# A decoder layer on one core: at two norm boundaries, 512 columns of x come at once and the rest in stages

## The chip, the cores and the metric

The kernel runs on one core of a Trainium2 chip. The time is that of one execution on the device, in microseconds (us), as the median of three runs. A profile is taken of one further execution.

## The reference

One layer of a decoder is computed for a batch of 1, 256 tokens, a width of 2048 and an FFN width of 5632, all in float32. Shortened to what matters:

```
h = rms_norm(x, ln_mix_pre)
proj = h @ w_in
o = heads(proj)
x = x + rms_norm(o @ w_out, ln_mix_post)
h = rms_norm(x, ln_ffn_pre)
g, u = split(h @ w_gate_up)
f = (silu(g) * u) @ w_down
x = x + rms_norm(f, ln_ffn_post)
gate = sigmoid(rms_norm(x, ln_pli) @ w_pli_gate)
x = x + gate * (p @ w_pli_proj)
```

Twice a norm over all 2048 columns lies between two matrix products: after w_out (the norm is added to x, and x is what w_gate_up multiplies) and after w_down (x is what w_pli_gate multiplies). These are called the FFN boundary and the gate boundary below. The scale of the norm ahead of a product is one number per token, so the kernel applies it to the product's result and multiplies only the gain into x.

## The kernel before

The 256 tokens are two tiles of 128 (t = 0 and 1). A product's accumulator is one PSUM bank of 128 tokens by 512 columns; there are eight banks. Every float32 operand is split into a high and a low part (`split`, L108: ScalarE casts the high part, VectorE subtracts it from the raw value), and a product of two is three matmuls: high by high, high by low, low by high. So one block of 128 rows of a weight costs three matmuls of 512 columns for each t.

Weights come from HBM on SyncE's queue into `wraw`, are split into `whi` and `wlo`, and each of these three has three buffers of 128x4x512. `gemm` (L178) with `Chunk` (L133) runs a product of 512 columns: chunks of four row blocks, with t = 0 and 1 taking turns every two row blocks; `front` chunks at the start and `tail` chunks at the end are run for t = 0 first and then for t = 1, so that t = 0 starts early or ends early.

The order on each engine is set by the Tile framework's scheduler: by default it follows the program's order; what is written under `tc.high_priority` is put ahead by the given number of places (200 for weight loads and their splits, 1000 for chains that end a product). The engines then run their lists in order and wait for each other through semaphores.

At a boundary `post_norm` (L243) runs for each t, from the last evacuation of the product (`evac_out`, L566, and `evac_down`, L810). VectorE multiplies the last 512 columns by the gain (L571 or L822), sums the squares (L246), GpSimd takes the power -1/2 (`rsqrt`, L216, tile `rs`), and then, for each of four groups of 512 columns: VectorE adds the normed product to x (L250), TensorE transposes the group in four matmuls against an identity (`split_T`, L235, into banks 4 and 5), VectorE multiplies by the next gain (L240), and ScalarE and VectorE split the result into `hT_hi` and `hT_lo` (L109 and L110). Each of these is 128x512. `hT` is what the next product multiplies; row blocks 0 to 3 of the weight need group 0, 4 to 7 group 1, and so on.

To give TensorE something to do meanwhile, half of p @ w_pli_proj is run at each boundary (`embed`, L590, two `gemm`s of two row blocks each: 24 matmuls, of `pT`). Its results are kept in memory (`pp_d`) until the end, and so is x (`x_d`, L605).

After the FFN boundary `unit_first` (L729) computes the first 512 of 5632 gate and up columns. Its weights come as `Pair` objects (L642): two row blocks of the gate columns and two of the up columns in one `whi`/`wlo` buffer. The first two pairs are run for t = 0 and then t = 1, the other six with both t. `differences` (L608) makes operands that only the later units use; its pieces are queued with `later` and released by `tick`. Ten more units (L755), and in three parts the products with w_down, follow. After the gate boundary come four `gemm`s of 512 columns with w_pli_gate, of 16 row blocks each, the first with one chunk of `front`, and `evac_gate` (L848), which ends in the output's stores.

Of the kernel before, what the change touches and what calls it, by code (L numbers as in the profile page):

```python
# [10 lines left out]
F32 = mybir.dt.float32  # L11
BF16 = mybir.dt.bfloat16
F32R = mybir.dt.float32r
# [4 lines left out]
T = 2  # L18
# [18 lines left out]
def kernel(  # L37
# [205 lines left out]
    def post_norm(hT, x_sb, t, ssy, gain):  # L243
# [4 lines left out]
        for c in range(4):  # L248
# [3 lines left out]
            split_T(hT, x_sb, t, c, gain)  # L252

# [4 lines left out]
    with tc.tile_pool(name="mixed", bufs=1) as mixed:  # L258
# [307 lines left out]
        def evac_out(n, last):  # L566
            def evac(t, pm):
# [21 lines left out]

    def embed(n, ring, out):  # L590

        gemm((pT_hi, pT_lo), w_pli_proj, 0, 2, n * NB, out, ring=ring)

    def embed_out(n):
        def evac(t, pm):
            pp = temp()
            nc.scalar.copy(pp, pm)
            nc.gpsimd.dma_start(out=pp_d[:, (2 * t + n) * NB:(2 * t + n + 1) * NB], in_=pp)
        return evac
# [42 lines left out]
    class Pair:  # L642


        def __init__(self, j, i, seven):
            self.i, self.seven = i, seven
            with tc.high_priority(offset=WEIGHT_AHEAD):
                raw, hi, lo = w_tiles()
                rows = slice(i * 2 * P, (i + 1) * 2 * P)
                for n0, sl in ((DFF + j * NB, slice(0, 4, 3)), (j * NB, slice(1, 3))):  # L650
                    nc.sync.dma_start(
                        out=raw[:, sl], in_=w_gate_up[rows, n0:n0 + NB].rearrange("(c q) n -> q c n", q=P))
# [41 lines left out]
        def first(self, m):  # L694

            t, n = {2: (0, 0), 3: (0, 1), 4: (1, 0), 5: (1, 1)}[m]
            return [([x[:, 2 * self.i + c, t, :] for x in hT], [x[:, k, :] for x in self.w])
                    for c, k in enumerate(((1, 2), (0, 3))[n])]
# [4 lines left out]
    def accumulate(m, terms, first, last):  # L703
        for x, (a, w) in enumerate(terms):
            for y, (u, v) in enumerate(((0, 0), (0, 1), (1, 0))):
                nc.tensor.matmul(  # L706
                    bank[M[m]], lhsT=a[u], rhs=w[v], start=first and x == 0 and y == 0,
                    stop=last and x == len(terms) - 1 and y == 2)

    def hidden(fT, k, t, f):  # L710
# [18 lines left out]
    def unit_first(j, fT, k):  # L729

        n = len(PAIRS)
        pairs = [Pair(j, i, False) for i in range(2)]
        for ms in ((2, 3), (4, 5)):
            for i in range(2):
                for m in ms:
# [189 lines left out]
```

## Time and profile before

| what | value |
|---|---|
| median of 3 runs | 1270.91 us (1270.76 to 1270.93) |
| the profiled execution's own time | 1270.12 us |
| its span, first to last instruction | 1268.4 us |
| TensorE (PE) busy | 1246.9 us, 98% |
| VectorE (DVE) busy | 828.6 us, 65% |
| ScalarE (ACT) busy | 613.7 us, 48% |
| GpSimd (POOL) busy | 28.3 us, 2% |
| DMA | 245.08 MB, 193 GB/s over the span |

The profiled execution's time is the span and 1.7 us around it. The times of the rows are us from the span's start. PE's busy share is high because matmuls overlap: a matmul's row lasts longer than the distance to the next one's start, so a stretch is best read by the starts of its matmuls. A row's "idle before" names the instruction that ended the wait.

### The profile page before, as it was taken

What the parts mean: (1) busy time and instruction counts of PE and PEld (TensorE: products, weight loads), DVE (VectorE), ACT (ScalarE), POOL (GpSimd) and SP (SyncE); (2) the same over time, 40 slices, a digit from 0 to 9 for tenths busy, and PEclk for the clock granted to TensorE, in tenths of its full rate; (3) what the DMA queues carried; (4) which work ended last, traced back from release to release, by engine and by line L of the source; (5) the groups of instructions that cost most, each with busy time, mean ns of one, the idle gap of its engine ahead of it and who ended that gap; (6) DMA issues with size and microseconds to landing.
All of it is one profiled execution on the core that took longest, in us unless ns stands there. A gap on an engine that the chain in (4) does not pass through costs nothing.

```text
span 1268.4 us, 14080 instructions
## 1 busy us (share of the span) xinstructions
PE 1246.9 (98%) x5554; PEld 1003.9 (79%) x5554; DVE 828.6 (65%) x812; ACT 613.7 (48%) x683; POOL 28.3 (2%) x53
## 2 busy tenths in 40 slices
PE   9999999999999899999999999999999999997998
PEld 6887888888887688888888888888888888886886
DVE  6574665555545957987535798886457988657543
ACT  6654554445443745555433555553334555446332
POOL 0001000000100100000000000000000000001000
PEclk9999999999999899999999999999999999998999
DMA  9754745454754655556555555556555555843661
GB/s 341 265 165 163 239 151 167 165 166 166 246 190 161 238 194 170 185 189 220 199 186 178 189 186 189 201 176 222 197 174 185 188 188 185 314 163 133 235 210 53
DMA packets 121810, 245.08 MB, mean 193 GB/s; under 512 B 6112, under 2 KB 6416, under 8 KB 120848
## 3 DMA queue, kind: packets, MB, share of 16 engines
q1 hardware_dynamic: 119536, 233.07, 54.4%
q0 software_dynamic: 1952, 11.02, 2.3%
q8 instruction: 43, 0.70, 0.2%
q14 instruction: 23, 0.19, 0.0%
q10 hardware_dynamic: 256, 0.10, 0.0%
HBM read 238.91 MB, written 6.83 MB: 194 GB/s over the span
## 4 chain that ended last, share of the span: by engine, by line
PE 93%; DVE 3%; ACT 2%; issue 1%; DMA 1%; POOL 0%; ACTq 0%; DVEq 0%; POOLq 0%
PE bank L159 52%; PE bank L706 37%; ACT whi L109 1%; DVE wlo L110 1%; PE bank L715 1%; PE bank L367 1%; DMA wraw<-in_w_in_dram 1%; PE bank L337 1%; DVE x_sb L250 0%; DVE hT_lo L110 0%; ACT hT_hi L109 0%; DMA gT<-in_gains_dram 0%; PE bank L380 0%; PE bank L379 0%; PE bank L378 0%
## 5 line engine op out<-in xcount | busy, mean ns | idle before, releaser
L110 DVE TENSOR_TENSOR wlo<-wraw,whi 128x2048 fp32r<-128x2048 f32 (+2 forms) x237 | 475.1, 2014 | 322.0 <-ACT whi L109 321.7
L109 ACT CAST whi<-wraw 128x2048 fp32r<-128x2048 f32 (+2 forms) x237 | 398.5, 1688 | 435.3 <-PE bank L159 250.6
L159 PE MATMUL bank<-whi,hT_hi 128*128 128x512 f32 x512 | 207.9, 407 | 1.1 <-ACT whi L109 1.1
L159 PE MATMUL bank<-wlo,hT_hi 128*128 128x512 f32 x512 | 203.5, 397 | 1.6 <-DVE wlo L110 1.5
L159 PE MATMUL bank<-whi,hT_lo 128*128 128x512 f32 x512 | 203.3, 397 | 0.0
L706 PE MATMUL bank<-wlo,hT_hi 128*128 128x512 f32 x454 | 180.8, 398 | 4.1 <-DVE wlo L110 4.1
L706 PE MATMUL bank<-whi,hT_lo 128*128 128x512 f32 x454 | 180.0, 397 | 0.0
L706 PE MATMUL bank<-whi,hT_hi 128*128 128x512 f32 x454 | 179.1, 399 | 0.3 <-ACT hT_hi L109 0.3
L159 PE MATMUL bank<-whi,fT_hi 128*128 128x512 f32 x352 | 139.8, 397 | 0.0
L159 PE MATMUL bank<-wlo,fT_hi 128*128 128x512 f32 x352 | 139.2, 395 | 0.0
L159 PE MATMUL bank<-whi,fT_lo 128*128 128x512 f32 x352 | 139.2, 395 | 0.0
L159 PEld LDWEIGHTS bank<-whi,hT_lo 128*128 128x128 f32 x512 | 96.8, 189 | 23.5 <-DVE hT_lo L284 0.2
L159 PEld LDWEIGHTS bank<-wlo,hT_hi 128*128 128x128 f32 x512 | 96.9, 189 | 22.8 <-DVE wlo L110 2.9
L159 PEld LDWEIGHTS bank<-whi,hT_hi 128*128 128x128 f32 x512 | 96.8, 189 | 22.7 <-ACT whi L109 1.6
L706 PEld LDWEIGHTS bank<-wlo,hT_hi 128*128 128x128 f32 x454 | 85.7, 189 | 26.1 <-DVE wlo L110 6.5
L706 PEld LDWEIGHTS bank<-whi,hT_lo 128*128 128x128 f32 x454 | 85.7, 189 | 20.3
L706 PEld LDWEIGHTS bank<-whi,hT_hi 128*128 128x128 f32 x454 | 85.5, 189 | 20.4 <-ACT hT_hi L109 0.5
L666 DVE TENSOR_TENSOR wlo<-wsum,whi 128x2048 fp32r<-128x2048 f32 x30 | 68.7, 2290 | 24.8 <-ACT whi L665 24.8
L159 PEld LDWEIGHTS bank<-whi,fT_lo 128*128 128x128 f32 x352 | 66.1, 188 | 16.0
L159 PEld LDWEIGHTS bank<-whi,fT_hi 128*128 128x128 f32 x352 | 66.1, 188 | 15.8
L159 PEld LDWEIGHTS bank<-wlo,fT_hi 128*128 128x128 f32 x352 | 66.2, 188 | 15.6
L159 PE MATMUL bank<-whi,oT_hi 128*128 128x512 f32 x128 | 51.2, 400 | 0.0
(166 smaller groups left out, 1329.4 us busy)
## 6 DMA issues: line engine op xcount, KB each, us to landing
wraw<-in_w_gate_up_dram SPq DMA_DIRECT2D x176, 512.0 KB, 4.8
wraw<-in_w_in_dram SPq DMA_DIRECT2D x40, 1024.0 KB, 5.2
wraw<-in_w_down_dram SPq DMA_DIRECT2D x33, 1024.0 KB, 5.0
wraw<-in_w_out_dram SPq DMA_DIRECT2D x16, 1024.0 KB, 5.0
wraw<-in_w_pli_gate_dram SPq DMA_DIRECT2D x16, 1024.0 KB, 5.1
wraw<-in_w_down_dram SPq DMA_DIRECT2D x22, 512.0 KB, 5.0
wraw<-in_w_in_dram SPq DMA_DIRECT2D x14, 512.0 KB, 8.7
y_sb<-in_xT_dram SPq DMA_DIRECT2D x8, 256.0 KB, 8.1
```

The lines of the kernel that those rows point to most:

```text
L109: nc.scalar.copy(hi, raw)
L110: nc.vector.tensor_tensor(lo, raw, hi.bitcast(F32), ALU.subtract)
L159: nc.tensor.matmul(self.pm[t], lhsT=a[:, c, t, :], rhs=b[:, c % KG, :], start=c == 0 and a is a_hi and b is hi, stop=c == self.nk - 1 and ...
L337: nc.tensor.transpose(out=pt[:, h * P:(h + 1) * P], in_=nat[:, h * P:(h + 1) * P], identity=ident)
L367: nc.tensor.matmul(out, lhsT=a[u], rhs=b[w], start=i == 0, stop=i == 2)
L666: nc.vector.tensor_tensor(slo, s, shi.bitcast(F32), ALU.subtract)
L706: nc.tensor.matmul(bank[M[m]], lhsT=a[u], rhs=w[v], start=first and x == 0 and y == 0, stop=last and x == len(terms) - 1 and y == 2)
L715: nc.tensor.transpose(out=pt[:, c * P:(c + 1) * P], in_=f[:, c * P:(c + 1) * P], identity=ident)
```

## The change

At both boundaries `post_norm` now does only group 0 of the columns, and keeps the other three as functions in `rest`. The sum of squares comes ahead of the multiplication by the gain (`finish`). The product that follows a boundary is run by a new function, `unit_plain`, which takes pairs of row blocks for two times 512 columns; after its first two pairs are done for t = 0 it does group 1 of x, after t = 1 group 2, and after its third pair group 3 and what needs all of x: the sums of squares (`token_rs`), the store to `x_d` and, at the FFN boundary, `differences` and the allocation of `fT`. Its last two pairs are run block by block, each block with its evacuation behind it. Three products use it: `unit_first`, p's projection (one pair for both column halves instead of two `gemm`s) and w_pli_gate (two runs of eight pairs instead of four `gemm`s; each weight load is 512 KB instead of 1024 KB). The number of matmuls is the same. The core of the diff:

```diff
-    def post_norm(hT, x_sb, t, ssy, gain):
+    def post_norm(hT, x_sb, t, ssy, gain, finish):
         s1 = small.tile([P, 1], F32, name="s1")
         nc.vector.tensor_reduce(s1, ssy, axis=mybir.AxisListType.X, op=ALU.add)
         r = rsqrt(s1, 1)
-        for c in range(4):
+        finish()
+
+        def columns(c):
             sl = slice(c * NB, (c + 1) * NB)
             nc.vector.scalar_tensor_tensor(
                 out=x_sb[:, t, sl], in0=y_sb[:, t, sl], scalar=r, in1=x_sb[:, t, sl], op0=ALU.mult, op1=ALU.add)
             split_T(hT, x_sb, t, c, gain)
+
+        columns(0)
+        for c in range(1, 4):
+            rest[c].append(lambda c=c: columns(c))
...
-                nc.vector.tensor_tensor(y_sb[:, t, sl], pm, gpost[:, sl], ALU.mult)
+                def scaled():
+                    nc.vector.tensor_tensor(y_sb[:, t, sl], pm, gpost[:, sl], ALU.mult)
                 if last:
-                    post_norm(hT, x_sb, t, ssy[t], G_FFN)
+                    post_norm(hT, x_sb, t, ssy[t], G_FFN, scaled)
...
-    for n in range(2):
-        embed(n, Ring(2, 3) if n == 0 else Ring(6, 7), embed_out(n))
-    rs = [token_rs(x_sb, t) for t in range(T)]
-    for t in range(T):
-        nc.gpsimd.dma_start(out=x_d[:, t * D:(t + 1) * D], in_=x_sb[:, t])
-    xs.close()
...
+    def unit_plain(aT, src, na, nb, np, banks, out, front=0, between={}):
+        order = [(t, n) for t in range(T) for n in range(2)]
+
+        def emit(t, n, pairs):
+            for w in pairs:
+                accumulate(bank[banks[t, n]], w.block(aT, t, n), w.i == 0, w.i == np - 1)
+
+        pairs = [Pair(src, na, nb, i) for i in range(front)]
+        for t in range(T if front else 0):
+            for w in pairs:
+                for n in range(2):
+                    emit(t, n, [w])
+            between.get(t, lambda: None)()
+        tail = min(2, np - front)
+        for i in range(front, np - tail):
+            w = Pair(src, na, nb, i)
+            for t, n in order:
+                emit(t, n, [w])
+            between.get(i, lambda: None)()
+            tick()
+        pairs = [Pair(src, na, nb, i) for i in range(np - tail, np)]
+        for t, n in order:
+            emit(t, n, pairs)
+            out(t, n, bank[banks[t, n]])
+        tick()
...
+        def normed():
+            rest_columns(3)
+            rs.extend(token_rs(x_sb, t) for t in range(T))
+            for t in range(T):
+                nc.gpsimd.dma_start(out=x_d[:, t * D:(t + 1) * D], in_=x_sb[:, t])
...
+            differences()
+
+        unit_plain(hT, w_gate_up, j * NB, DFF + j * NB, len(PAIRS), FIRST, out, front=2,
+                   between={0: lambda: rest_columns(1), 1: lambda: rest_columns(2), 2: normed})
...
+    embed(0, {(0, 0): 2, (0, 1): 3, (1, 0): 6, (1, 1): 7}, embed_out)
...
-    for n in range(4):
-        gemm(hT, w_pli_gate, 0, KC, n * NB, evac_gate(n), front=1 if n == 0 else 0, tail=1 if n == 3 else 0,
-             ring=Ring(7, 0) if n % 2 == 0 else Ring(3, 6))
+    unit_plain(hT, w_pli_gate, 0, NB, KC // 2, {(0, 0): 3, (0, 1): 0, (1, 0): 6, (1, 1): 1}, evac_gate(0), front=2,
+               between={0: lambda: rest_columns(1), 1: lambda: rest_columns(2), 2: normed})
+    unit_plain(hT, w_pli_gate, 2 * NB, 3 * NB, KC // 2, {(0, 0): 2, (0, 1): 7, (1, 0): 4, (1, 1): 5}, evac_gate(1))
```

How the scheduler now orders the instructions is seen best at three places. In these rows a line number is that of the program it stands in; in the changed program L235 is still the transpose, L240 and L110 the operations of `split_T` and `split`, and the addition to x (before L250) is L252, the scaling by the gain (L571) L586, the sum of squares L246, the matmul of a pair (L706) L705.

TensorE at the FFN boundary, from the last matmul of p's projection on, before:

```order
L159 MATMUL bank_76<-whi,pT_lo 128x512
L706 MATMUL bank_69<-whi,hT_hi 128x512
L706 MATMUL bank_72<-whi,hT_hi 128x512
L235 MATMUL bank_73<-ident,x_sb 128x128 x4
L706 MATMUL bank_70<-whi,hT_hi 128x512
L706 MATMUL bank_71<-whi,hT_hi 128x512
L235 MATMUL bank_74<-ident,x_sb 128x128 x8
L706 MATMUL bank_69<-wlo,hT_hi 128x512
L706 MATMUL bank_69<-whi,hT_lo 128x512
```

and in the changed program, at the first place where x's group 1 is transposed, which is behind the 24 matmuls of the first two pairs for t = 0 (`bank_73` and `bank_74` hold the transposes of t = 0 and 1, `bank_69` and `bank_71` are t = 0's accumulators, `bank_70` and `bank_72` those of t = 1):

```order
L705 MATMUL bank_71<-whi,hT_hi 128x512
L705 MATMUL bank_71<-wlo,hT_hi 128x512
L705 MATMUL bank_71<-whi,hT_lo 128x512
L235 MATMUL bank_73<-ident,x_sb 128x128 x4
L235 MATMUL bank_74<-ident,x_sb 128x128 x4
L705 MATMUL bank_70<-whi,hT_hi 128x512
L705 MATMUL bank_70<-wlo,hT_hi 128x512
L705 MATMUL bank_70<-whi,hT_lo 128x512
```

Before, all transposes stood ahead of all but four matmuls of the next product. Now groups 1, 2 and 3 of both t stand in pairs between blocks of 24 matmuls of that product.

VectorE at the FFN boundary, from the end of t = 0's last product on (`rs_2987` and `rs_2986` belong to t = 0, `rs_3037` and `rs_3012` to t = 1), before:

```order
L571 TENSOR_TENSOR y_sb<-bank_69,gpost 128x512
L246 TENSOR_REDUCE s_2985<-ss 128x1
L213 MEMSET ss 128x1
L250 SCALAR_TENSOR_TENSOR x_sb<-y_sb,rs_2987,x_sb 128x512 x3
L240 TENSOR_TENSOR y_sb<-bank_73,gT 128x512
L571 TENSOR_TENSOR y_sb<-bank_70,gpost 128x512
L246 TENSOR_REDUCE s_3035<-ss 128x1
L240 TENSOR_TENSOR y_sb<-bank_74,gT 128x512
L250 SCALAR_TENSOR_TENSOR x_sb<-y_sb,rs_3037,x_sb 128x512
L110 TENSOR_TENSOR hT_lo<-y_sb,hT_hi 128x4x128 x2
```

and in the changed program:

```order
L246 TENSOR_REDUCE s_2984<-ss 128x1
L586 TENSOR_TENSOR y_sb<-bank_69,gpost 128x512
L252 SCALAR_TENSOR_TENSOR x_sb<-y_sb,rs_2986,x_sb 128x512 x2
L246 TENSOR_REDUCE s_3010<-ss 128x1
L586 TENSOR_TENSOR y_sb<-bank_70,gpost 128x512
L240 TENSOR_TENSOR y_sb<-bank_73,gT 128x512
L252 SCALAR_TENSOR_TENSOR x_sb<-y_sb,rs_3012,x_sb 128x512
L110 TENSOR_TENSOR wlo<-wraw,whi 128x2048
L110 TENSOR_TENSOR hT_lo<-y_sb,hT_hi 128x4x128
L240 TENSOR_TENSOR y_sb<-bank_74,gT 128x512
```

The sum of squares has moved ahead of the scaling, and a weight split (`wlo`, 128x2048) now stands in the midst of group 0, where before the weight splits stood behind nearly all of the groups.

GpSimd's queue at the gate boundary (`pp` are the loads of p's kept products, `rs_7781` and `rs_7832` before, `rs_7775` and `rs_7802` now, are the power for t = 0 and 1), before:

```order
L808 DMA x_sb_7385<-x_d 128x2048 x2
L218 TENSOR_TENSOR rs_7781<-s_7779,mhalf 128x1
L843 DMA pp_7870<-pp_d 128x512
L843 DMA pp_7871<-pp_d 128x512
L843 DMA pp_7874<-pp_d 128x512
L843 DMA pp_7875<-pp_d 128x512
L218 TENSOR_TENSOR rs_7832<-s_7830,mhalf 128x1
```

and in the changed program:

```order
L848 DMA x_sb_7380<-x_d 128x2048 x2
L889 DMA pp_7817<-pp_d 128x512
L889 DMA pp_7818<-pp_d 128x512
L218 TENSOR_TENSOR rs_7775<-s_7773,mhalf 128x1
L889 DMA pp_7821<-pp_d 128x512
L889 DMA pp_7822<-pp_d 128x512
L218 TENSOR_TENSOR rs_7802<-s_7800,mhalf 128x1
```

Two of the four loads have moved ahead of t = 0's power, and all four ahead of t = 1's as before.

## Rows read from the trace of the kernel before

**Rows 1.** The page, parts 1 and 4: busy time of the engines (share, instructions); the chain that ended last

```profile
PE 1246.9 (98%) x5554; PEld 1003.9 (79%) x5554; DVE 828.6 (65%) x812; ACT 613.7 (48%) x683; POOL 28.3 (2%) x53
...
PE 93%; DVE 3%; ACT 2%; issue 1%; DMA 1%; POOL 0%; ACTq 0%; DVEq 0%; POOLq 0%
```

**Rows 2.** Waits of PE, whole span: line waited for, us in total, times, longest us

```profile
PE bank L235 <- DVE x_sb L250: 7.5, 5, 3.2
PE bank L706 <- DVE wlo L110: 4.1, 1, 4.1
```

**Rows 3.** Stretches: length; PE, PEld, DVE, ACT, POOL busy us; granted clock, DMA share, GB/s

```profile
335.04:405.05 70.01, 70.01 (x301) 56.38 (x301) 32.33 (x21) 27.24 (x27) 0.59 (x1) 1.00 0.62 215
407.43:428.19 20.76, 14.34 (x69) 11.08 (x69) 20.56 (x29) 17.64 (x33) 3.85 (x7) 0.84 0.56 208
1154.57:1175.67 21.10, 14.57 (x64) 10.93 (x64) 20.80 (x30) 17.38 (x33) 2.52 (x5) 0.76 0.29 96
```

**Rows 4.** Timeline of PE, FFN boundary: start us, us, line, operation, names, count [idle before]

```profile
408.11 0.66 PE L235 MATMUL bank<-ident,x_sb 128*128 128x128 f32 x4 [0.51 <-DVE x_sb L250]
...
410.20 0.60 PE L235 MATMUL bank<-ident,x_sb 128*128 128x128 f32 x4
...
410.87 0.39 PE L159 MATMUL bank<-whi,pT_lo 128*128 128x512 f32 x1
...
420.33 0.66 PE L235 MATMUL bank<-ident,x_sb 128*128 128x128 f32 x4 [1.56 <-DVE x_sb L250]
...
425.07 0.80 PE L706 MATMUL bank<-wlo,hT_hi 128*128 128x512 f32 x1 [4.09 <-DVE wlo L110]
...
426.09 0.63 PE L706 MATMUL bank<-whi,hT_hi 128*128 128x512 f32 x1
...
426.52 0.63 PE L706 MATMUL bank<-wlo,hT_hi 128*128 128x512 f32 x1
```

**Rows 5.** Timeline of DVE, FFN boundary, same columns

```profile
406.46 0.15 DVE L246 TENSOR_REDUCE s<-ss 128x1 f32<-128x5 f32 x1
...
407.30 2.08 DVE L250 SCALAR_TENSOR_TENSOR x_sb<-y_sb,rs,x_sb 128x512 f32<-128x512 f32 x3 [0.57 <-POOL rs L218]
```

**Rows 6.** Groups by shape, 405 to 430 us: busy us, mean ns of one, idle before

```profile
L110 DVE TENSOR_TENSOR wlo<-wraw,whi 128x2048 fp32r<-128x2048 f32 x3 | 6.8, 2283 | 0.0
...
L250 DVE SCALAR_TENSOR_TENSOR x_sb<-y_sb,rs,x_sb 128x512 f32<-128x512 f32 x8 | 5.7, 745 | 0.6 <-POOL rs L218 0.6
...
L240 DVE TENSOR_TENSOR y_sb<-bank,gT 128x512 f32<-128x512 f32 x8 | 5.4, 681 | 0.0
...
L110 DVE TENSOR_TENSOR hT_lo<-y_sb,hT_hi 128x512 fp32r<-128x512 f32 x8 | 5.3, 684 | 0.1
```

**Rows 7.** Timeline of PE, gate boundary, columns as in Rows 4

```profile
1153.64 0.39 PE L159 MATMUL bank<-whi,fT_lo 128*128 128x512 f32 x1
...
1157.81 0.60 PE L235 MATMUL bank<-ident,x_sb 128*128 128x128 f32 x4
1158.16 0.48 PE L159 MATMUL bank<-wlo,pT_hi 128*128 128x512 f32 x1
...
1169.90 1.11 PE L235 MATMUL bank<-ident,x_sb 128*128 128x128 f32 x4 [3.25 <-DVE x_sb L250]
```

**Rows 8.** Timeline of POOL, gate boundary, same columns

```profile
1153.72 0.56 POOL L218 TENSOR_TENSOR rs<-s,mhalf 128x1 f32<-128x1 f32 x1 [66.38 <-DVE s L246]
1154.34 2.18 POOL L843 DMA_DIRECT2D pp<-pp_d  x4
```

**Rows 9.** Stretches, columns as in Rows 3

```profile
408.00:418.00 10.00, 9.63 (x53) 7.74 (x54) 9.85 (x18) 8.90 (x14) 2.77 (x5) 1.00 0.30 119
600.00:800.00 200.00, 200.00 (x871) 161.07 (x870) 135.94 (x102) 93.86 (x76) 0.00 (x0) 1.00 0.55 185
```

**Rows 10.** DMA issues: line, queue, count, KB each, median us from issue to landing

```profile
wraw<-in_w_gate_up_dram SPq DMA_DIRECT2D x176, 512.0 KB, 4.8
...
wraw<-in_w_pli_gate_dram SPq DMA_DIRECT2D x16, 1024.0 KB, 5.1
```

More of the change, by code (lines that the diff above doesn't have):

```diff
@@ L252, in post_norm, with rest_columns @@
             split_T(hT, x_sb, t, c, gain)
+        columns(0)
+        for c in range(1, 4):
+            rest[c].append(lambda c=c: columns(c))
+    rest = {c: [] for c in range(1, 4)}
+    def rest_columns(c):
+        for f in rest[c]:
+            f()
+        rest[c].clear()
     x_d = dram.tile([P, T * D], F32, name="x_d")
@@ L701, with accumulate @@
     ps_f = Ring(7)
-    def accumulate(m, terms, first, last):
+    def accumulate(pm, terms, first, last):
         for x, (a, w) in enumerate(terms):
@@ L706, in accumulate, with hidden @@
                 nc.tensor.matmul(
[L707 removed]
+                    pm, lhsT=a[u], rhs=w[v], start=first and x == 0 and y == 0,
                     stop=last and x == len(terms) - 1 and y == 2)
[L710 removed]
+    def hidden(k, t, f):
         def run():
@@ new lines, with evac_down, evac, scaled @@
+    for part, (j0, j1) in enumerate(parts):
+        for j in range(j0, j1):
+            (unit if j else unit_first)(j, j - j0)
+        if part == 2:
+            hx.close()
+            xs2 = ctx.enter_context(tc.tile_pool(name="xs2", bufs=1, side="right", reuse_waits="tile"))
+            gpost = xs2.tile([P, D], F32, name="gpost2")
+            x_sb = xs2.tile([P, T, D], F32, name="x_sb2")
+            nc.gpsimd.dma_start(out=gpost, in_=ln_ffn_post.broadcast_to([P, D]))
+            for t in range(T):
+                nc.gpsimd.dma_start(out=x_sb[:, t], in_=x_d[:, t * D:(t + 1) * D])
+        def evac_down(n, part):
+            def evac(t, pm):
+                sl = slice(n * NB, (n + 1) * NB)
+                if part == 0:
+                    nc.scalar.copy(y_sb[:, t, sl], pm)
+                    return
+                nc.vector.tensor_tensor(y_sb[:, t, sl], y_sb[:, t, sl], pm, ALU.add)
+                if part == 1:
+                    return
+                nc.scalar.activation(
+                    out=junk, in_=y_sb[:, t, sl], func=AF.Square, scale=1.0 / math.sqrt(D),
+                    accum_out=ssy[t][:, n:n + 1])
+                def scaled():
+                    nc.vector.tensor_tensor(y_sb[:, t, sl], y_sb[:, t, sl], gpost[:, sl], ALU.mult)
+                if n == 3:
+                    post_norm(hT, x_sb, t, ssy[t], G_PLI, scaled)
+                else:
+                    scaled()
+            return evac
+        nk = (j1 - j0) * 4
+        def finish_hidden(g):
+            while g == nk // 2 - 2 and pending:
+                tick()
+            return 1
+        for n in range(4):
+            gemm(fT, w_down, j0 * 4, nk, n * NB, evac_down(n, part), tail=1 if part == 2 and n == 3 else 0,
+                 ring=(Ring(4, 5), Ring(6, 0), Ring(1, 2), Ring(3, 6))[n], before=finish_hidden if n == 0 else None)
@@ L843, with evac_gate, out @@
             nc.gpsimd.dma_start(out=pp[t][n], in_=pp_d[:, (2 * t + n) * NB:(2 * t + n + 1) * NB])
-    for n in range(2, 4):
-        embed(n, Ring(7, 0) if n == 2 else Ring(1, 2), lambda t, pm: nc.scalar.copy(pp[t][n], pm))
-    rs = [token_rs(x_sb, t) for t in range(T)]
-    def evac_gate(n):
-        def evac(t, pm):
+    embed(2 * NB, {(0, 0): 0, (0, 1): 1, (1, 0): 2, (1, 1): 7},
+          lambda t, n, pm: nc.scalar.copy(pp[t][2 + n], pm))
+    rs = []
+    def evac_gate(half):
+        def out(t, n, pm):
+            n += 2 * half
             pieces = 2 if n == 3 and t == 1 else 1
```

122 lines of the change are left out of this document (42 added, 80 removed).

## The prediction

> **What bounds the kernel.** The page comes first. TensorE is busy 98% of the span and is 93% of the chain that ended last; apart from its own weight loads, which overlap, no other engine is above 65% [rows 1]. So a change counts only as far as it shortens TensorE's work or the time in which TensorE waits. Its work stays the same: the order of the changed program has as many matmuls and transposes as before. What is left is its idle time, and the list of its waits says where that is: the two largest entries are transposes that wait for the addition to x (7.5 us in five waits) and pair matmuls that wait for a weight split (4.1 us in one) [rows 2]. Both belong to the two norm boundaries, so these are the stages to look at.
>
> Third, the undisturbed price. In 335.04 to 405.05 us TensorE ran 301 rows, one of which had begun before, in 70.01 us: 0.2334 us per matmul at granted clock 1.00 [rows 3]. A group of four transposes is priced by its distance to what follows: with one matmul it took from 410.20 to 410.87, 0.67 us [rows 4], so 0.44 by itself.
>
> Fourth, the two stretches. At the FFN boundary 20.76 us pass [rows 3]. Of its 69 rows one began before and 32 are transposes, so 36 matmuls (8.40 us) and 8 groups (3.52 us) are work: **8.84 us are lost**. At the gate boundary 21.10 us pass with 64 rows, so 31 matmuls (7.24 us) and 3.52 us of transposes: **10.34 us are lost**. In all 19.2 us.
>
> The timeline shows two kinds of loss. One is waiting: 0.51, 1.56 and 4.09 us at the FFN boundary [rows 4], up to 3.25 us at the gate [rows 7]. The other follows from it: matmuls come 0.43 us apart after the long wait (426.09 to 426.52 [rows 4]), the lower of the clock's two levels (1.2 GHz instead of 2.4), and the granted clock of the stretches is 0.84 and 0.76 [rows 3]. Without the idle time the second loss should go too.
>
> Why TensorE waits is seen on VectorE. One group of x for one t costs it an addition (745 ns), a gain (681 ns) and a low part (684 ns) [rows 6]: 2.1 us, and eight groups 16.9 us. Ahead of them TensorE has 24 matmuls of p and four of the next product, 28 x 0.2334 = 6.5 us. VectorE is therefore some 10 us behind, and the weight split (2.28 us [rows 6]) stands behind all that: TensorE's 4.09 us.
>
> **The change part by part.** *Staging.* The product now needs only group 0 at once: 2 x 2.1 = 4.2 us of VectorE for both t, against 24 matmuls of p, 5.6 us. Groups 1, 2 and 3 are due each after another 24 matmuls (5.6 us), which the changed order shows as transposes of group 1 behind 24 matmuls. Per such block VectorE has 4.2 us of x and 2.3 us of a weight split, 6.5 us: 0.9 more than the block. But the second front pair is split at the start of the boundary, and group 3's block is followed by pairs that need only a split, 2.3 of 5.6 us. Over six blocks (33.6 us) VectorE has 12.7 us of x and five splits of 2.28, 24.1 in all. So the backlog is at most some 2 us deep in mid-stage, and a group is added to x well before its transposes. I take no wait there.
>
> *The first group.* Here is little slack, so each t is walked. At the FFN boundary the sum of squares was reduced at 406.46, behind a scaling of a 128x512 tile (0.6 us by its likes in [rows 6], counting overlap); now it goes ahead. The power lands 0.57 us after the reduction's end plus hops, the addition began at 407.30 [rows 5], so it now begins at 406.7 and ends at 407.4 instead of 408.1. The transposes of t = 0 stand behind two of p's matmuls, at 407.9: the 0.51 us wait goes. For t = 1 I walk to 0.15 us at most. t = 0's low part stands behind the weight split and ends at about 413.6; its first user comes at 414.5, so 0.9 us are left. At the gate, the last matmul of w_down starts at 1153.64 [rows 7]; the power took 0.56 us and then four loads of p's products 2.18, 0.55 each [rows 8]. Two of these now stand ahead of the power: 1.1 us. They write where w_down's operand lay, so they start when that matmul has ended, at 1154.04: 1154.04 + 1.1 + 0.56 + 0.745 [rows 6], and the addition to x ends at about 1156.5. TensorE has 12 matmuls of p until 1156.6: 0 to 0.2 us of wait. The high part of t = 0 is ready about 0.15 us late at the first gate matmul. I put the residue of both boundaries at **0.7 us**; its bounds are 0 and, if both loads' 1.1 us are wholly exposed in addition, 1.8.
>
> *The rest of the gate's edits.* Sixteen loads of 1 MB become 32 of half the size. The FFN stage already lives on such loads: 200.00 busy of 200 us at 185 GB/s, granted clock 1.00 [rows 9], each landing after 4.8 us against 5.1 for the large [rows 10]. Nothing is charged, and the end stays as it was: 12 matmuls of the last block, then the same evacuation. The pairing of p's projection moves no matmul count. The cover for all of VectorE's moved work is the matmul stream itself; what is late next, should a group slip, is its weight split, at 2.28 us.
>
> *Sum*, against the profiled execution's own 1270.12: 1270.12 - 8.84 - 10.34 + 0.7 = 1251.6. The median of the runs stands 0.79 above that execution, so **1252.4 us**. Bounds: a group of transposes is cheapest where the next matmul starts 0.35 us behind it (1157.81 to 1158.16 [rows 7]); all sixteen at that price are 16 x 0.09 = 1.4 less than at 0.44, and without residue and without the median's offset that makes 1270.12 - 19.2 - 1.4 = 1249.5. With the residue at its upper bound it is 1253.5.
>
> **Rivals.** *VectorE stays the bound (0.14).* If the backlog is deeper than I count (splits and groups compete on one in-order engine, and VectorE and ScalarE were already busy nearly all of both stretches [rows 3]), each boundary keeps one wait between 1.56 and 4.09 [rows 4], say 2.8 us, and behind it some 8 matmuls at the lower clock, 8 x (0.43 - 0.2334) = 1.6 us. Twice 4.4 in place of my 0.7 is 8.1 more: 1260.5; at one boundary only, 1256.4. For it: 6.5 us of VectorE against blocks of 5.6. Against: the six-block count.
>
> *The waits only move (0.03).* The next product could wait at its third or fourth pair as long as it now does at its first. Then all 19.2 us return: about 1271. Against: the changed order itself, where the transposes stand 24 matmuls apart and no group precedes more than one split. This is also where the case belongs that the change does not do what it says.
>
> *The clock is held low by the scattered transposes (0.03).* Before, 64 rows of transposes stood close together; now a pair of groups breaks the matmuls every 5.6 us. If that kept the granted clock at its lower level from the first to the last transpose, 94 matmuls per boundary (22 of p's and three blocks of 24) would cost 0.193 more each: 188 x 0.193 = 36 us, and the time would be about 1288, slower than before. It decides once 99 matmuls (19.2 / 0.193) run at the lower level. Against: between 408 and 418 us, groups of transposes stood among matmuls and the granted clock was 1.00 [rows 9]; the lower level was seen only behind several us of waiting. The Trainium skill (TensorE: Matmul & The Clock Gate, Part 4: PE-mode transpose) says that transposes do not count as busy time for the clock as matmuls do. By that rule the stretch from 408 to 418, with the groups of 408.11 and 410.20 in it [rows 4], was in danger too; the trace does not bear that out.
>
> **How the numbers follow.** My case has 0.80, the rivals 0.14, 0.03 and 0.03. What a measurement of this kernel can tell from no change is 0.2%, 2.5 us. The first two cases are faster by far more than that: 0.94. The third is no change: 0.03; the fourth is slower: 0.03. The range runs from 1249.5 (no residue, the cheaper transposes, the runs' offset gone) to 1260.0, which takes in the first rival up to nearly its middle; left out are its deeper half and the two small cases, some 0.13.
>
> **What would show it.** In the changed profile TensorE's waits for the addition to x and for pair splits should be below 1 us together at each boundary; the granted clock should be 1.00 in every stretch of 10 us from 400 to 445 us and over the 40 us behind the last w_down matmul; the span should be 1250; the pairs of groups should be followed by a matmul within 1 us of their start. VectorE should be nearly filled for 30 us behind each boundary, without TensorE waiting. Wrong would be: a wait over 1.5 us at a group's transposes or at a weight split (VectorE's bound), matmul starts 0.43 us apart without an idle time ahead of them (the clock), or the first addition to x at the gate later than 1157 (GpSimd's loads).

## The result, and the profile after

The changed kernel takes **1252.35 us** (median of 4 runs, 1251.37 to 1252.79), the kernel before 1270.92 on the same chip: a ratio of 0.9851, 95% interval 0.9833 to 0.9868. The profiled execution is the run of 1252.79 us, its span 1251.1.

The page of the changed kernel, its first and fourth part:

```profile
PE 1242.5 (99%) x5554; PEld 1001.5 (80%) x5554; DVE 828.5 (66%) x810; ACT 613.1 (49%) x681; POOL 28.6 (2%) x53
...
PE 97%; DVE 1%; ACT 1%; issue 1%; DMA 0%; DVEq 0%; ACTq 0%
```

TensorE still has 5554 rows, as in [rows 1], but it is 99% busy and 97% of the last chain. Its list of waits over the whole span holds three lines now, all ahead of the FFN boundary (columns as in [rows 2]; gaps of more than 0.15 us are listed):

```profile
PE bank L204 <- DVE junk L201: 1.3, 1, 1.3
PE bank L159 <- ACT whi L109: 1.2, 1, 1.2
PE bank L452 <- DVE sps L445: 0.4, 1, 0.4
```

Both lines of [rows 2] are gone. Two stretches, one from the last w_out matmul on and one from the last w_down matmul on (columns as in [rows 3]):

```profile
408.19:428.90 20.71, 20.71 (x103) 16.90 (x102) 18.15 (x26) 16.92 (x30) 4.41 (x8) 1.00 0.84 288
1145.55:1175.55 30.00, 29.97 (x144) 23.70 (x143) 26.89 (x34) 22.30 (x37) 4.74 (x8) 1.00 0.63 211
```

At the FFN boundary TensorE is busy all of the 20.71 us with 103 rows, where [rows 3] had 69 in 20.76, and the granted clock is 1.00 at both boundaries instead of 0.84 and 0.76.

Two marks split the span in every kernel of this study: the start of the last w_out matmul (where transposes stand ahead of one of the last matmuls, the start of the last one ahead of them, plus 0.23 for each that follows) and the start of the last w_down matmul. The span is given to 0.1 us, so the last column holds to about 0.05.

| profile | start to w_out mark | w_out to w_down mark | w_down mark to end |
|---|---|---|---|
| before | 407.43 | 746.21 | 114.76 |
| changed | 408.20 | 737.35 | 105.55 |
| difference | +0.77 | -8.86 | -9.21 |

The sum, -17.30, is the difference of the spans (1268.4 - 1251.1). The first part is nearly the same program in all kernels. It ended between 406.85 and 408.39 in the 14 profiles, which is more than most of the effects below. So small effects are read from the other two columns.

VectorE's timeline in the changed kernel, at the FFN boundary (columns as in [rows 5]):

```profile
404.97 2.29 DVE L110 TENSOR_TENSOR wlo<-wraw,whi 128x2048 fp32r<-128x2048 f32 x1 [3.31 <-ACT whi L109]
407.18 0.15 DVE L246 TENSOR_REDUCE s<-ss 128x1 f32<-128x5 f32 x1
...
408.02 1.42 DVE L252 SCALAR_TENSOR_TENSOR x_sb<-y_sb,rs,x_sb 128x512 f32<-128x512 f32 x2
...
411.34 2.28 DVE L110 TENSOR_TENSOR wlo<-wraw,whi 128x2048 fp32r<-128x2048 f32 x1
```

The split at 404.97 belongs to the first pair of the next product. It stands *ahead of* the boundary. This is the row that the experiments turned out to be about. In the kernel before the corresponding VectorE rows are:

```profile
403.35 1.23 DVE L110 TENSOR_TENSOR wlo<-wraw,whi 128x1024 fp32r<-128x1024 f32 x1 [4.37 <-ACT whi L109]
...
422.74 2.28 DVE L110 TENSOR_TENSOR wlo<-wraw,whi 128x2048 fp32r<-128x2048 f32 x1
```

There the split of 403.35 is half as wide (128x1024, half of p's projection), and the first pair's split comes at 422.74, behind nearly all the work on the groups of x.

### The profile page after: what moved, and what is told of

Same layout as the page of the kernel before. It is cut to its first block, busy times and chain, and to the rows that moved or that the text cites. A ratio compares the mean times of both kernels' runs of the same rounds, so it can differ in the third digit from the quotient of the medians.

```text
span 1251.1 us, 14098 instructions
## 1 busy us (share of the span) xinstructions
PE 1242.5 (99%) x5554; PEld 1001.5 (80%) x5554; DVE 828.5 (66%) x810; ACT 613.1 (49%) x681; POOL 28.6 (2%) x53
## 4 chain that ended last, share of the span: by engine, by line
PE 97%; DVE 1%; ACT 1%; issue 1%; DMA 0%; DVEq 0%; ACTq 0%
PE bank L159 47%; PE bank L705 46%; PE bank L714 1%; PE bank L380 1%; PE bank L235 1%; PE bank L350 1%; ACT whi L109 1%; DVE wlo L110 0%; DMA gT<-in_gains_dram 0%; PE bank L393 0%; PE bank L392 0%; PE bank L391 0%; PE bank L418 0%; PE bank L488 0%; DVE tmp L442 0%
## 5 line engine op out<-in xcount | busy, mean ns | idle before, releaser
L110 DVE TENSOR_TENSOR wlo<-wraw,whi 128x2048 fp32r<-128x2048 f32 (+3 forms) x235 | 474.8, 2030 | 308.3 <-ACT whi L109 307.8
L109 ACT CAST whi<-wraw 128x2048 fp32r<-128x2048 f32 (+3 forms) x235 | 398.1, 1700 | 421.7 <-PE bank L159 211.2
L705 PE MATMUL bank<-wlo,hT_hi 128*128 128x512 f32 x582 | 230.2, 396 | 0.0
L705 PE MATMUL bank<-whi,hT_hi 128*128 128x512 f32 x582 | 230.0, 398 | 0.0
L705 PE MATMUL bank<-whi,hT_lo 128*128 128x512 f32 x582 | 229.8, 395 | 0.0
L705 PEld LDWEIGHTS bank<-wlo,hT_hi 128*128 128x128 f32 x582 | 109.2, 188 | 27.4 <-DVE wlo L110 2.2
L705 PEld LDWEIGHTS bank<-whi,hT_lo 128*128 128x128 f32 x582 | 109.2, 188 | 26.4 <-DVE hT_lo L110 0.2
L705 PEld LDWEIGHTS bank<-whi,hT_hi 128*128 128x128 f32 x582 | 109.2, 188 | 26.0 <-ACT hT_hi L109 0.4
L159 PEld LDWEIGHTS bank<-whi,fT_lo 128*128 128x128 f32 x352 | 66.1, 188 | 16.1
```

The source lines that it names most:

```text
L109: nc.scalar.copy(hi, raw)
L110: nc.vector.tensor_tensor(lo, raw, hi.bitcast(F32), ALU.subtract)
L159: nc.tensor.matmul(self.pm[t], lhsT=a[:, c, t, :], rhs=b[:, c % KG, :], start=c == 0 and a is a_hi and b is hi, stop=c == self.nk - 1 and ...
L705: nc.tensor.matmul(pm, lhsT=a[u], rhs=w[v], start=first and x == 0 and y == 0, stop=last and x == len(terms) - 1 and y == 2)
```

## The experiments

Each ratio is to the kernel before on the same chip. That kernel's medians were 1270.83 to 1272.19 us there, so the times of runs from different chips compare to about 1 us.

### Staging undone, one boundary at a time, and halved

The edit is one number in `post_norm`: `4 if gain == G_FFN else 1`, `4 if gain == G_PLI else 1`, and `2`.

```diff
-        columns(0)
-        for c in range(1, 4):
+        now = 4 if gain == G_FFN else 1
+        for c in range(now):
+            columns(c)
+        for c in range(now, 4):
             rest[c].append(lambda c=c: columns(c))
```

> The changed kernel with all four groups of x done at once at the FFN boundary only. Theory (the gain is the staging, and each boundary has its own): the 8.8 us lost at this boundary come back, with the earlier sum of squares kept some 0.5 us less, so 8.3 to 8.8 more than the changed kernel's 1252.35: 1260.7 to 1261.2. Transposes should wait for the addition to x and a pair matmul for its weight split, with a stretch at the lower granted clock behind that; the gate boundary should look as in the changed kernel. Rival (the gain came from the pairs or from the earlier sum of squares): below 1254. Rival (waits only move between the boundaries): the gate boundary would gain what this one loses, time near 1252.

> The changed kernel with all four groups at once at the gate boundary only. Theory: the 10.3 us lost there come back less the 1.1 us that the changed kernel still loses there, 9.2 more: 1261.6. Rival (pairs or earlier sum): below 1254. If the two boundaries are independent, this run and the one with the FFN boundary at once together add up to the 18.6 us between the kernels.

> The changed kernel with two groups of x at once at both boundaries and two in stages. Theory (a backlog on VectorE that grows with the groups that stand ahead of the product): the two groups cost 8.4 us of VectorE and one weight split 2.3 may come between, against 5.6 us of p's matmuls, so a wait of 2.8 to 5.1 us per boundary and up to 1.6 us of lower clock behind it: 3 to 6 us each, 1258 to 1264. Rival (only the first addition to x matters, the rest is hidden by the matmuls whatever its order): no wait, 1252 to 1253. Rival (any group ahead of the product that is not needed costs as all do): 9 us each, 1270.

Measured: 1252.84 us with all groups at once at the FFN boundary (ratio to before 0.9854, 0.9839 to 0.9869), 1254.48 at the gate (0.9868, 0.9853 to 0.9883), 1251.54 with two groups at once (0.9842, 0.9826 to 0.9858). The theory of the prediction had asked for 1261, 1261.6 and 1258 to 1264. It fell in all three. With all four groups at once TensorE's waits at that boundary, FFN at once first and gate at once second, are:

```profile
PE bank L707 <- DVE wlo L110: 0.7, 1, 0.7
```

```profile
PE bank L707 <- DVE wlo L110: 1.5, 1, 1.5
...
PE bank L707 <- ACT hT_hi L109: 0.5, 1, 0.5
PE bank L235 <- DVE x_sb L252: 0.5, 1, 0.5
```

The long waits of [rows 2] do not return: the longest is 0.7 us at the FFN boundary, where the kernel before waited 4.09, and 1.5 at the gate, where it waited 3.25. By the marks, FFN at once costs 1.07 us (738.42), gate at once 2.11 (107.66). VectorE has the same eight groups to do as in the kernel before, yet TensorE works on. The split of 404.97 (404.08 in this run) is what it has to work on.

### What p's projection has to do with it

The weights have three buffers. Before, p's projection took two of them, one per column half, each half filled. Now both halves share one. So a new theory: either remedy suffices, a buffer free early enough for the next product's first pair to be split ahead of the groups, or few groups ahead of that split. Four kernels make the table complete: p in two products again (`gemm` for each column half in `embed`) with x staged, the same with x at once (`now = 4`), p as one pair with x at once, and the kernel before with p's pair alone:

```diff
 def embed(na, banks, out):
-        unit_plain((pT_hi, pT_lo), w_pli_proj, na, na + NB, 1, banks, out)
+        for n in range(2):
+            gemm((pT_hi, pT_lo), w_pli_proj, 0, 2, na + n * NB, lambda t, pm, n=n: out(t, n, pm),
+                 ring=Ring(banks[0, n], banks[1, n]))
```

In the kernel before:

```diff
-        gemm((pT_hi, pT_lo), w_pli_proj, 0, 2, n * NB, out, ring=ring)
+        with tc.high_priority(offset=WEIGHT_AHEAD):
+            raw, hi, lo = w_tiles()
+            for i in range(2):
+                nc.sync.dma_start(
+                    out=raw[:, 2 * i:2 * i + 2],
+                    in_=w_pli_proj[0:2 * P, (n + i) * NB:(n + i + 1) * NB].rearrange("(c q) n -> q c n", q=P))
+            split(hi, lo, raw)
...
```

> The changed kernel, x in stages, but p's projection again as two products with a weight buffer each. The at-once runs brought back only 0.5 and 2.1 us, so staging is not alone what gained. New theory (either of two things suffices: a buffer that is free before the boundary, so that the next product's first weight pair is split ahead of the groups of x; or few groups ahead of that split): with staging alone the first pair's split stands behind some 5 us of group 0, a wait of 1 to 2 us per boundary: 1253 to 1257. Rival (p in one buffer is the whole gain, staging does nothing): 1268 to 1271. Rival (neither; the earlier sum of squares or the order of the product does it): 1252.

> The changed kernel with both undone: all groups of x at once, and p's projection as two products. Theory (either suffices): with neither, the loss is back, 1267 to 1271, the long wait being again the one for the first pair's weight split, behind nearly all groups. Rival (the earlier sum of squares or the order of the product does it): below 1257.

> The changed kernel with all groups of x at once at both boundaries, p's projection as one pair. The two boundaries undone singly gave 0.5 and 2.1 more; if they are independent, 1252.35 + 2.6 = 1255.0 under every theory now held. Much above that, 1260 or more, would mean that one boundary's staging covers for the other's.

> The kernel before with one edit alone: p's projection reads its two column halves from one weight buffer instead of two. Nothing of x is staged, the sum of squares stays where it was, and the products with gate, up and w_pli_gate are as before. Theory (a buffer free before the boundary suffices): most of the gain, 1254 to 1258; the first pair's split should stand ahead of the boundary and the wait of 4.1 us for it be gone. Rival (staging is needed): 1268 to 1271.

| us (ratio to before, 95% interval) | p in one buffer | p in two buffers |
|---|---|---|
| x staged | 1252.35 (0.9833 to 0.9868), the change | 1252.76 (0.9841 to 0.9870) |
| x at once | 1255.90 (0.9865 to 0.9895) | 1270.68 (0.9984 to 1.0003) |

With neither remedy the loss is all there: 1270.68, no different from before, and the two columns are 746.4 and 114.6 us as in the kernel before, though the product's new order, the earlier sum of squares and the pairs for w_pli_gate are all in it. These are worth nothing that shows by themselves. With either one most of it is gone: staging alone leaves nothing that shows (the 1 to 2 us of wait that were expected for it did not come, its list has 0.3 us at the gate), p's pair with x at once leaves 3.6 us (1255.90, near the 1255.0 to which the two boundaries undone singly add up). In the kernel before, p's pair as the only edit gives 1256.38 (0.9883, 0.9867 to 0.9900), 15 of the 18.6 us, with no staging anywhere.

No run gave the weights a fourth buffer and left p's projection as it was. That it is the buffer is read from ScalarE's and VectorE's timelines. The high part of the first pair's split needs a free buffer. ScalarE, kernel before, then the kernel before with p's pair:

```profile
402.27 1.05 ACT L109 CAST whi<-wraw 128x1024 fp32r<-128x1024 f32 x1 [4.55 <-PE bank L159]
...
409.68 1.91 ACT L109 CAST whi<-wraw 128x2048 fp32r<-128x2048 f32 x1
```

```profile
403.04 1.91 ACT L109 CAST whi<-wraw 128x2048 fp32r<-128x2048 f32 x1 [3.69 <-PE bank L159]
...
409.29 1.89 ACT L109 CAST whi<-wraw 128x2048 fp32r<-128x2048 f32 x1
```

Before, the 128x1024 cast at 402.27 is p's second half, and the first pair's cast comes at 409.68, behind the w_out mark, when w_out's last chunk no longer needs its buffer. With p's pair the first pair is cast at 403.04, in the buffer that p's second half took. At the gate the same happens: the first split of w_pli_gate starts at 1169.76, 16.1 us behind the w_down mark, in the kernel before, and at 1143.58, 3.2 us ahead of it, with p's pair. VectorE with p's pair alone, with staging alone, and with neither:

```profile
404.98 2.29 DVE L110 TENSOR_TENSOR wlo<-wraw,whi 128x2048 fp32r<-128x2048 f32 x1 [3.31 <-ACT whi L109]
...
408.63 1.41 DVE L250 SCALAR_TENSOR_TENSOR x_sb<-y_sb,rs,x_sb 128x512 f32<-128x512 f32 x2 [0.57 <-POOL rs L218]
```

```profile
412.42 2.28 DVE L110 TENSOR_TENSOR wlo<-wraw,whi 128x2048 fp32r<-128x2048 f32 x1
```

```profile
422.52 2.28 DVE L110 TENSOR_TENSOR wlo<-wraw,whi 128x2048 fp32r<-128x2048 f32 x1
```

With neither, the split is ready to run by 412.5 (its high part was cast from 410.60, 1.91 us) and VectorE does it ten us later, behind nearly all of x. TensorE waits for it:

```profile
419.98 0.66 PE L235 MATMUL bank<-ident,x_sb 128*128 128x128 f32 x4 [1.44 <-DVE x_sb L252]
...
424.85 0.79 PE L707 MATMUL bank<-wlo,hT_hi 128*128 128x512 f32 x1 [4.22 <-DVE wlo L110]
```

### Only the order of that split

In the kernel before, one number at two places: the load and split of the first pair, and (in `Chunk.load`, not shown) of w_pli_gate's first chunk, get 3000 places of priority instead of 200.

```diff
-            with tc.high_priority(offset=WEIGHT_AHEAD):
+            with tc.high_priority(offset=3000 if j == 0 and i == 0 else WEIGHT_AHEAD):
                 raw, hi, lo = w_tiles()
```

> The kernel before with one number changed at two places: the load and split of the first weight set behind each boundary (pair 0 of gate and up; the first chunk of w_pli_gate) get a priority above the groups of x. P's projection keeps its two buffers, x comes at once. Theory (what costs is the place of that split on VectorE, behind the groups; the buffer matters only because it decides that place): pair 0's split starts near 412 instead of 422.7, the 4.1 us wait goes, and the groups of x come 2.3 us later, behind which TensorE has pair 0 to run: 1254 to 1260. Rival (a buffer must come free before the boundary, order alone does nothing): 1267 to 1271. Rival (the groups pushed back by the split make the transposes wait as long): 1267 to 1271 too, with the waits at the transposes instead of the split.

Measured: 1261.17 us (0.9913, 0.9896 to 0.9930). The split moved as meant, and the wait for it went. ScalarE's cast for it first, then VectorE's splits, then TensorE:

```profile
408.69 1.91 ACT L109 CAST whi<-wraw 128x2048 fp32r<-128x2048 f32 x1 [3.21 <-PE bank L159]
```

```profile
410.81 2.29 DVE L110 TENSOR_TENSOR wlo<-wraw,whi 128x2048 fp32r<-128x2048 f32 x1
...
423.71 2.28 DVE L110 TENSOR_TENSOR wlo<-wraw,whi 128x2048 fp32r<-128x2048 f32 x1
```

```profile
426.05 0.80 PE L706 MATMUL bank<-wlo,hT_hi 128*128 128x512 f32 x1 [2.15 <-DVE wlo L110]
```

The cast, now first in its line, starts at 408.69, as TensorE lets go of the buffer with the last w_out matmul (408.18 to 408.65): with p in two buffers the first split cannot come ahead of the boundary, whatever its priority. It stands between the groups. The second pair's split, at 423.71, is still behind them, and TensorE waits 2.15 us for that one at a later point, with the granted clock at 0.50, the lower level, from 426 to 429 us. So order alone gives 11 of the 18.6 us; 1254 to 1260 had been expected. A split between the groups delays those behind it by its 2.3 us. One that is over by 407.27, as with p's pair, delays the first addition to x by some 0.55 us (408.63, 0.42 behind the w_out mark of 408.21, against 0.13 ahead of it before).

### The first group's terms

Two terms of the prediction concern the first group. The scaling was put back ahead of the sum of squares:

```diff
+        finish()
         s1 = small.tile([P, 1], F32, name="s1")
...
         r = rsqrt(s1, 1)
-        finish()
```

> The changed kernel with the scaling by the gain ahead of the sum of squares, as before. Theory (the first group has little slack): the first addition to x comes 0.6 us later; at the FFN boundary, where the first transposes started 0.13 us behind the end of that addition, they should wait 0.4 to 0.5 us; at the gate boundary the power waits for GpSimd's two loads anyway, so 0.1 to 0.2 us. Time 1252.8 to 1253.1, to be read from the trace rather than from the time. Rival (the first group has slack of its own): no wait in either place, 1252.35.

It took 1252.59 us in its one run. The first addition to x starts 0.42 us behind the w_out mark (407.27 - 406.85) instead of 0.18 ahead of it, 0.6 later as expected. The transposes wait 0.33 us, for t = 1 though and not for t = 0, and 0.16 at the gate. The stretch from mark to mark is 0.94 us longer (738.29; the four profiles with the FFN stage of the change lie between 737.34 and 737.40), the last one 105.76. So the earlier sum is worth about 1 us at the FFN boundary and nothing that shows at the gate.

At the gate the prediction charged GpSimd's loads of p's kept products. They were first moved behind `token_rs` in the program, then also to SyncE's queue:

```diff
-    for t in range(T):
-        for n in range(2):
-            nc.gpsimd.dma_start(out=pp[t][n], in_=pp_d[:, (2 * t + n) * NB:(2 * t + n + 1) * NB])
...
     def normed():
         rest_columns(3)
         rs.extend(token_rs(x_sb, t) for t in range(T))
+        for t in range(T):
+            for n in range(2):
+                nc.sync.dma_start(out=pp[t][n], in_=pp_d[:, (2 * t + n) * NB:(2 * t + n + 1) * NB])
```

> The changed kernel with the four loads of p's kept products behind the gate boundary's powers on GpSimd's queue. The prediction charged these loads with the gate's residue, 1.1 us of loads ahead of the first power. In the changed kernel's trace that power starts 0.4 us after the sum it needs, since two loads run until then. Theory (loads cost what they delay): the first addition to x comes 0.4 to 0.5 us earlier, the gate boundary loses some 0.3 to 0.5 us less: 1251.9 to 1252.1, to be read from the stretch behind the last w_down matmul (105.55 us now). Rival (they are hidden, and the weight split that stands between the addition and its gain causes the gate's residue): 105.4 to 105.6 again. Rival (they carry the whole residue): 104.5.

> The changed kernel with the four loads of p's kept products issued on SyncE's queue among the weight loads of the gate stage instead of on GpSimd's (the earlier try moved them later in the program only, and its trace still shows two of them ahead of the first power). Theory (they delay the first power by 0.4 us, and that is part of the gate's residue): the first power follows the sum at once, the first addition to x starts 0.4 to 0.5 us earlier behind the last w_down matmul (2.24 us behind its start in the changed kernel, 1.8 now), and the 105.55 us behind that matmul become 105.0 to 105.2. Rival (another wait takes over, the residue stays): 105.5. Rival (the loads carry the residue): 104.5. In the time at most 1 us, 1251.4 to 1252.4.

The first try (1252.43 us; 0.9848, 0.9833 to 0.9863) tells nothing: the scheduler put two of the loads ahead of the power as before. The second (1251.99; 0.9847, 0.9833 to 0.9860) took them off. GpSimd in the changed kernel, then with the loads on SyncE:

```profile
1146.01 1.08 POOL L889 DMA_DIRECT2D pp<-pp_d  x2 [66.77 <-PE bank L159]
1147.11 0.65 POOL L218 TENSOR_TENSOR rs<-s,mhalf 128x1 f32<-128x1 f32 x1
```

```profile
1146.93 0.87 POOL L218 TENSOR_TENSOR rs<-s,mhalf 128x1 f32<-128x1 f32 x1 [67.63 <-DVE s L246]
```

The power starts 0.22 us earlier behind the w_down mark (1.34 instead of 1.56) but lasts 0.87 instead of 0.65, and the first addition to x starts at the same distance, 2.24 us (1147.79 and 1147.83). By the trace of the changed kernel alone the loads seem to hold up the power, which follows them at once. Without them the addition comes no earlier, so they cost nothing. The last stretch is 105.11, within the 105.0 to 105.2 expected, but not for the reason expected; kernels with the same gate stage as the change gave 105.17 (FFN at once) and 105.55, so the 0.44 between them is no effect.

### Room on VectorE

Behind each staged group of each t, four sums over its 512 columns were added, which nothing reads.

```diff
...
         for c in range(1, 4):
             rest[c].append(lambda c=c: columns(c))
+            rest[c].append(lambda c=c: extra(x_sb[:, t, c * NB:(c + 1) * NB]))
```

> The changed kernel with extra work for VectorE that nothing reads: behind each staged group of x and each t four sums over its 512 columns, 24 of some 0.6 us per boundary, 14.6 us. It measures how much room the staged order leaves on VectorE. The prediction's count (24.1 of 33.6 us used) leaves 9.5 us: 14.6 - 9.5 = 5.1 us of wait per boundary and up to 1.6 of lower clock, 1262 to 1266. A count by due times (group 2 is due at pair 4, 28 us behind the boundary, with 24.7 us of work ahead of it) leaves 3.3 us there: 6.4 to 11.3 per boundary, 1265 to 1278. Rival (VectorE was at its limit): 14.6 per boundary, 1282. Rival (room for all of it): 1252.

1257.38 us in its one run. At the gate the extra 14.6 us cost nothing (105.16). From w_out to w_down mark they cost 5.3 us (742.63), but not where any of the counts placed it: TensorE is full in the 40 us behind the FFN boundary, not in the next 40. With the load, then the first of these stretches in the changed kernel (columns as in [rows 3]):

```profile
407.00:447.00 40.00, 40.00 (x190) 32.49 (x189) 39.36 (x50) 22.44 (x28) 4.41 (x8) 1.00 0.62 202
447.00:487.00 40.00, 36.09 (x155) 27.76 (x154) 35.75 (x47) 22.80 (x31) 1.66 (x2) 1.00 0.54 191
```

```profile
407.00:447.00 40.00, 40.00 (x190) 32.46 (x189) 34.46 (x49) 26.25 (x41) 5.77 (x10) 1.00 0.74 246
```

In the changed kernel VectorE has 5.5 of these 40 us left (39.36 busy with the load against 34.46), so some 10 us of the load do not fit. The backlog was carried on and came out at the first pairs of the second unit, as waits for casts and splits (1.99 us the longest). At the gate the load was hidden, at the FFN boundary there was room for a third of it in these 40 us. In both stages TensorE stayed full: without the load VectorE is not their bound, but at the FFN boundary it is not far from it.

## Why the prediction was right in its number and only half right in its cause

**The loss was sized rightly.** 8.84 us at the FFN boundary: measured 8.86. 10.34 at the gate less a residue: 9.21, so a residue of 1.1 there and none at the FFN boundary, where 0.7 was taken for both. 1252.4 against 1252.35. One of the bounds was misread. The 0.35 us of the cheapest group is not its whole price: in the kernel before, the matmul behind that group starts at 1158.16 and the one behind that at 1158.48, 0.32 us on instead of 0.23, so the group costs 0.44 as well. The lower end of the range took off 1.4 us that were not to be had.

**The cause was half of it.** Staging does by itself what the prediction said: with p's projection in two products as before, the time is 1252.76. What failed is the diagnosis under *Staging*: it put the whole 19.2 us down to a VectorE that was some 10 us behind because all eight groups stood ahead of the product. The runs show that eight groups at once cost only 3.6 us (1255.90) once p's projection leaves a buffer free. That "the second front pair is split at the start of the boundary" stood in the text as a help to staging; that the first is split ahead of it, and why, did not, and of the pairing it was said that it "moves no matmul count". It moves no matmul, but it moves a weight split from 422.7 to 405. VectorE was late with x as counted, but that alone makes TensorE wait little: with the first pair split early, TensorE runs its blocks between the transposes. It waited so long because the split stood behind the groups as well. The two remedies overlap: each alone gives about 15 us or more of 18.6. That the sum came out right while the effect was given to one of them is partly luck: it asked only that the loss go, by whatever remedy. The count for the stages was short, too: in the 33.6 us from 414.90 on VectorE was busy 27.42 us, not 24.1. It left out the pieces of `differences`, some 4.2 us in that stretch.

**The first group.** The walk had the addition to x begin 0.6 us earlier at the FFN boundary. It did not: 0.18 us ahead of the mark now (408.02 against 408.20), 0.13 before (407.30 against 407.43 [rows 5]). The first pair's split, 2.29 us from 404.97 on, stands ahead of the sum, which starts as it ends (407.18). The earlier sum pays for that delay, as the run with the old order shows. At the gate the addition ends 2.99 us behind the mark (1148.54 - 1145.55; the walk had 2.86), but not through GpSimd's loads. The sum itself comes late: VectorE is in the first pair's split from 1142.33 on, turns to t = 0's last evacuation only at 1144.54, and has t = 0's sum behind t = 1's evacuation, which waits for the last matmul. VectorE at the gate, changed kernel:

```profile
1142.33 2.29 DVE L110 TENSOR_TENSOR wlo<-wraw,whi 128x2048 fp32r<-128x2048 f32 x1 [3.31 <-ACT whi L109]
1144.54 0.68 DVE L856 TENSOR_TENSOR y_sb<-y_sb,bank 128x512 f32<-128x512 f32 x1
1145.98 0.69 DVE L856 TENSOR_TENSOR y_sb<-y_sb,bank 128x512 f32<-128x512 f32 x1 [0.77 <-PE bank L159]
1146.59 0.15 DVE L246 TENSOR_REDUCE s<-ss 128x1 f32<-128x5 f32 x1
...
1147.79 0.75 DVE L252 SCALAR_TENSOR_TENSOR x_sb<-y_sb,rs,x_sb 128x512 f32<-128x512 f32 x1 [0.46 <-POOL rs L218]
1148.46 2.29 DVE L110 TENSOR_TENSOR wlo<-wraw,whi 128x2048 fp32r<-128x2048 f32 x1
```

The split of the second pair at 1148.46 stands between the first addition and its gain. With two groups at once the scheduler put it behind both gains, and the last stretch was 104.57 instead of 105.11 to 105.80. That this split is the gate's residue fits, but no run moved it alone. Some 0.6 us of the residue show as gaps too short for the list, around t = 1's transposes, whose addition comes behind the split (1152.48): TensorE's rows at 1152.06, 1153.28 and 1153.88 start 0.40, 0.42 and 0.60 us behind the one before, where 0.23, 0.23 and 0.36 are undisturbed.

**The rivals.** *VectorE stays the bound*: no wait at either boundary in the list above, and the stages stayed full even with 14.6 us more for VectorE. *The waits only move*: no. *The clock held low by scattered transposes*: the granted clock is 1.00 in both stretches, with a pair of groups behind every 24 matmuls. TensorE, FFN boundary, such a pair:

```profile
420.27 0.40 PE L705 MATMUL bank<-whi,hT_lo 128*128 128x512 f32 x1
420.51 1.03 PE L235 MATMUL bank<-ident,x_sb 128*128 128x128 f32 x8
421.30 0.48 PE L705 MATMUL bank<-whi,hT_hi 128*128 128x512 f32 x1
421.62 0.39 PE L705 MATMUL bank<-wlo,hT_hi 128*128 128x512 f32 x1
```

The two groups take 0.79 us up to the next matmul, and that one 0.32 instead of 0.23 up to the one behind it: 0.88 us, 0.44 a group, as the prediction priced them. The Trainium skill's sentence that transposes do not count as busy time for the clock as matmuls do (TensorE: Matmul & The Clock Gate, Part 4: PE-mode transpose) had no price here: with a pair of groups behind every 24 matmuls the clock stayed at its upper level.

**The 512 KB loads** and the end cost nothing that shows: the last stretch is within the residue.

Of the kernels tried, two groups at once has the lowest median, 1251.54 us. Its interval (0.9826 to 0.9858) overlaps that of the change, so it is not shown to be faster.

## What to carry to other kernels

When an engine waits at a boundary for a weight split, look first at which buffer that weight is waiting for and who holds it. Here products of 24 matmuls, one at each boundary, that filled two of three buffers by half cost some 15 us together. When a change does two things that could each remove a wait, undoing one shows little and proves nothing about the other; all four combinations are needed. And compare small effects from mark to mark: here the start alone varied by 1.5 us between profiles.

## What was not expected of the hardware

The same waits can cost different amounts. The kernels with the gate at once and with both at once have the same gate stage and nearly the same waits there: 0.48, 0.45 and 1.55 us in one, 0.49, 0.45 and 1.54 in the other. Thirty us from the w_down mark on, gate at once first, both at once second:

```profile
1145.10:1175.10 30.00, 27.52 (x133) 21.67 (x132) 26.15 (x35) 20.41 (x37) 4.75 (x8) 1.00 0.51 175
```

```profile
1145.70:1175.70 30.00, 27.52 (x126) 21.55 (x126) 26.15 (x35) 20.08 (x36) 4.75 (x8) 0.94 0.50 175
```

The granted clock was 1.00 in one and 0.94 in the other, where matmuls then came 0.43 us apart for some 3 us:

```profile
1164.82 0.70 PE L707 MATMUL bank<-wlo,hT_hi 128*128 128x512 f32 x1 [1.54 <-DVE wlo L110]
1165.32 0.63 PE L707 MATMUL bank<-whi,hT_lo 128*128 128x512 f32 x1
1165.74 0.63 PE L707 MATMUL bank<-whi,hT_hi 128*128 128x512 f32 x1
```

The last stretch took 107.66 and 109.25 us. So waits of this size sometimes bring the lower level behind them and sometimes not, which is worth 1.6 us here. It does not look to be the kernel that decides: of the four runs of each, three have a granted clock of 1.000 over the whole run, and the slowest has 0.998 (1255.58 us with the gate at once; 1256.66 with both, which is the one profiled). What does decide it was not tried.
